# The modulation product of the second block: split float32r matmuls replaced by plain float32 matmuls on four 32-column strips

## The chip, the cores and the metric

The kernel runs on one core of a Trainium2 chip. The metric is the device time of one execution in microseconds (us); the time of a kernel is the median of its runs.

## What is computed

Two transformer-like blocks run one after the other on 256 tokens of width 1024, in float32. The second block has two layers, and each begins with a modulation: a vector `c` for the tokens and a vector `c_ctx` for the context are multiplied by a 1024 x 3072 matrix, and the result is cut into shift, scale and gate.

```python
for l in range(DEPTH):                                   # 2 layers
    mod_l = jax.nn.silu(c) @ w_ada[l] + b_ada[l]
    sh_l, sc_l, gt_l = jnp.split(mod_l[:, None, :], 3, axis=-1)
    mod_c = jax.nn.silu(c_ctx) @ w_ada[l] + b_ada[l]
    sh_c, sc_c, gt_c = jnp.split(mod_c, 3, axis=-1)
    h_l = _rmsnorm(x, g_pre[l]) * (1.0 + sc_l) + sh_l
    h_c = _rmsnorm(xc, g_pre[l]) * (1.0 + sc_c) + sh_c
    ...
    x = x + gt_l * _rmsnorm(out_l, g_post[l])
```

So the modulation is a product with two rows on the left and 24 MB of weights on the right (12 MB a layer). Nothing of the first block enters it, so it can be done at any time before the second block needs it.

## The kernel before

Matrix products run on TensorE with float32r operands. To keep precision, a weight tile of 1 MB (a unit: 128 partitions x 2048 floats) is loaded by one DMA into a buffer `raw` (three of these exist), ScalarE copies it as float32r (`hi`, L274) and VectorE subtracts that copy from the raw weights (`lo`, L275). Each half of a unit has its own `hi` and `lo` tile, of which four each exist. The activations are split in the same way, and `mm3` (L291 to L293) makes each product from three matmuls.

The modulation of one layer is the generator `ada` (L929). It works in 12 steps of 1 MB of weights, 24 for both layers: `product` (L937) takes 512 columns and 512 rows of `w_ada`, splits them as any other unit, and multiplies with `cvec`, four columns wide, namely hi and lo of the two vectors. These are eight matmuls, four with `lo` (L945) and four with `hi` (L946), each 512 columns wide with four stationary columns; the sum over the two halves of the rows and the bias are added by VectorE (L947). Eight steps make shift and scale; then small float32 matmuls with a selection matrix (L953) sum the rows and turn them into columns. Four steps make the gate, each second one followed by a float32 matmul with the selection matrix (L969), and the gate rows go to DRAM (L972).

What sets the order: these steps are pieces of filler. The first block (`block1`) yields a price of latency at each of its own steps, and the loop in `run` takes filler steps, each with a price in TensorE time, until the latency is paid. Eight modulation steps thus lie in the first 80 us among the first projections (reads of `in_e_w_in`), the other sixteen between 230 and 375 us, one after each unit of the first feed-forward (reads of `in_w_ff1` and `in_w_ff2`). A scheduler then fixes the order on each engine and the buffer that each tile gets; the order does not change during a run. All loads are issued by SyncE's queue (SP), in order: a load that waits for its buffer holds up the loads behind it.

Of the kernel before, what the change touches and what calls it, by code (L numbers as in the profile page):

```python
# [10 lines left out]
F32 = mybir.dt.float32  # L11
# [3 lines left out]
OP = mybir.AluOpType  # L15
# [12 lines left out]
# ---------------------------------------------------------------- constants that depend on shapes alone  # L28
# [26 lines left out]
# microseconds of other work that a step of the filler or of the background waits for, and its pace  # L55
# [26 lines left out]
def make_consts():  # L82
# [12 lines left out]
    # attention masks for [query, 256 keys] with queries 128..255  # L95
# [12 lines left out]
    # block 2 rope: [token, 128] in natural layout, halves of 32 inside each 64  # L108
# [10 lines left out]
    sel = np.zeros((100, 8), f)  # L119
    for q in range(4):  # L120
        for r in range(4):
            sel[32 * q + r, 2 * q + r % 2] = 1
# [4 lines left out]
# column-layout vectors (one value per partition), packed side by side  # L127
# [9 lines left out]
# row vectors that are spread over all partitions  # L137
# [10 lines left out]
def layout(inp):  # L148
    """Copies of the inputs in the layouts that the kernel loads; no arithmetic."""
# [22 lines left out]
    bada = np.zeros((2, 3, 4, 1024), np.float32)  # L172
    bada[:, :, 0] = a["b_ada_2"].reshape(2, 3, 1024)
    bada[:, :, 1] = a["b_ada_2"].reshape(2, 3, 1024)
    o["bada"] = bada
    for n in ("x", "e_w_in", "e_w_uq", "e_w_ukv", "e_w_out", "o_w_in", "o_w_out", "w_ff1", "w_ff2",
              "w_ple_gate", "w_ple_proj", "ctx_2", "w_ada_2", "w_in_2", "w_br_conv_2",
              "w_br_attn_2", "w_br_gla_2", "w_out_2", "g_post_2"):
# [8 lines left out]
class Pair:  # L187
    """x as hi + lo, both float32r, with the contraction index on partitions: [128, chunks, 256 tokens]."""
# [5 lines left out]
class Kern:  # L194
# [12 lines left out]
    # ------------------------------------------------------------ small helpers  # L207
# [24 lines left out]
    def load_consts(self):  # L232
# [7 lines left out]
        self.sel = g("sel", [100, 8])  # L240
# [39 lines left out]
    def tr_mm(self, ps, hi, lo, x, tick=False):  # L280
        """ps [128, 2, 256] = (columns of the unit) x (tokens)."""
# [38 lines left out]
    def gemm_tr(self, x, w, c0, cb, nk=8, width=256):  # L320
        """[256 columns of w as 2 x 128 partitions, 256 tokens]; cb(psum [128, 2, 256])."""
# [43 lines left out]
    def transposed(self, nat, nk, evac):  # L365
        """nat [128 tokens, 2, nk*128] -> evac(c0, n, psum [128, n, 256]) for runs of up to 2 chunks."""
# [9 lines left out]
    def square(self, h, ms, b, t, scr):  # L376
        """half b's part of the mean square of token tile t of h into ms[:, b, t]."""
# [10 lines left out]
    def raw_pair(self, h, gain):  # L388
        """h [128, 2, 1024] with a gain per column, transposed, as a pair: what follows scales by the rms norm's factor."""
# [1412 lines left out]
```

## Time and profile before

| | before |
|---|---|
| median of 3 runs | 2158.41 us (2156.14 to 2159.87) |
| profiled execution, span | 2158.8 us |
| TensorE (PE) busy | 2126.8 us, 99% |
| VectorE (DVE) busy | 1574.5 us, 73% |
| ScalarE (ACT) busy | 1167.1 us, 54% |
| splits of weights on DVE (L275), 620 | 748.3 us |
| splits of weights on ACT (L274), 620 | 641.5 us |
| matmuls of the modulation (L945, L946), 192 | 78.3 us of records, pipelined |

The profiled execution is as long as the median of the runs to within 0.4 us. How to read it: PE is the engine that is nearly always busy, but its records overlap: a matmul's record reaches to the end of its pipeline, so what one costs in a stream is the distance from its start to the next start, not the length of its record.

### The profile page before, as it was taken

To read this page: it belongs to the slowest core of one execution; us is meant where nothing else is said; L and a number is where in the kernel's file an instruction comes from. 1 tells how busy PE (TensorE), PEld (TensorE's weight loads), DVE (VectorE), ACT (ScalarE), POOL (GpSimd) and SP (SyncE) were. 2 spreads that over 40 slices of the span, in tenths; PEclk is the share of its full clock that TensorE was granted. 3 is DMA by queue.
4 is the path that set the end of the run, shared out by engine and by line. 5 is a ranking of instruction groups with operands and counts; after the bars stand their busy time and mean duration, and the time that the engine had idled before them with its cause. 6 is when DMAs were issued, how large, how long until landed. Compare 5 with 4: busy or idle time off the path is not lost.

```text
span 2158.8 us, 34589 instructions
## 1 busy us (share of the span) xinstructions
PE 2126.8 (99%) x13622; PEld 1881.5 (87%) x13622; DVE 1574.5 (73%) x2891; ACT 1167.1 (54%) x1838; POOL 9.2 (0%) x43
## 2 busy tenths in 40 slices
PE   7999999999999999999999999999999999999998
PEld 5788877888899988989998888889899988989997
DVE  7975787667766666898898577447878677667676
ACT  5754665455555445666565445434545445747553
POOL 0000000000000000000000000000000000000000
PEclk9999999999999999999999999999999999999999
DMA  8654687555435555754543343578876641425694
GB/s 262 221 167 150 220 276 261 186 177 191 149 106 174 195 189 182 248 185 134 187 132 117 112 136 121 166 241 277 282 237 193 206 139 58 141 84 164 204 314 175
DMA packets 290121, 397.06 MB, mean 184 GB/s; under 512 B 12658, under 2 KB 189138, under 8 KB 289574
## 3 DMA queue, kind: packets, MB, share of 16 engines
q1 hardware_dynamic: 289958, 394.85, 56.1%
q8 instruction: 107, 1.75, 0.3%
q14 instruction: 56, 0.46, 0.1%
HBM read 362.78 MB, written 32.03 MB: 183 GB/s over the span
## 4 chain that ended last, share of the span: by engine, by line
PE 90%; DVE 5%; ACT 3%; DMA 1%; issue 1%; SPq 0%; DVEq 0%; ACTq 0%
PE mm L292 25%; PE mm L293 25%; PE mm L291 25%; DVE wlo L275 2%; PE tp L1581 2%; PE at L1599 1%; PE at L1416 1%; PE at L1530 1%; PE mm L945 1%; PE mm L946 1%; PE at L576 1%; PE tp L1433 1%; ACT whi L274 1%; PE at L291 1%; PE tp L550 1%
## 5 line engine op out<-in xcount | busy, mean ns | idle before, releaser
L275 DVE TENSOR_TENSOR wlo<-raw,whi 128x1024 fp32r<-128x1024 f32 (+2 forms) x620 | 748.3, 1212 | 301.5 <-ACT whi L274 299.4
L274 ACT CAST whi<-raw 128x1024 fp32r<-128x1024 f32 (+2 forms) x620 | 641.5, 1041 | 472.9 <-PE mm L293 387.7
L291 PE MATMUL mm<-xh,wlo 128*128 128x256 f32 (+2 forms) x2048 | 621.1, 303 | 0.3 <-ACT xh L399 0.3
L292 PE MATMUL mm<-xl,whi 128*128 128x256 f32 (+2 forms) x2048 | 619.8, 303 | 0.9 <-DVE xl L400 0.9
L293 PE MATMUL mm<-xh,whi 128*128 128x256 f32 (+2 forms) x2048 | 618.3, 302 | 0.0
L291 PEld LDWEIGHTS mm<-xh,wlo 128*128 128x128 f32 (+1 forms) x2048 | 383.2, 187 | 16.1 <-ACT xh L399 0.5
L292 PEld LDWEIGHTS mm<-xl,whi 128*128 128x128 f32 (+1 forms) x2048 | 383.3, 187 | 15.5 <-DVE xl L400 1.1
L293 PEld LDWEIGHTS mm<-xh,whi 128*128 128x128 f32 (+1 forms) x2048 | 383.2, 187 | 14.2
L291 PE MATMUL mm<-whi,xl 128*128 128x512 f32 (+3 forms) x704 | 268.4, 383 | 3.1 <-ACT whi L274 2.9
L292 PE MATMUL mm<-wlo,xh 128*128 128x512 f32 (+3 forms) x704 | 269.4, 383 | 1.1 <-DVE wlo L275 1.1
L293 PE MATMUL mm<-whi,xh 128*128 128x512 f32 (+3 forms) x704 | 267.0, 380 | 0.0
L292 PE MATMUL mm<-pl,whi 128*128 128x256 f32 x576 | 160.9, 279 | 0.0
L293 PE MATMUL mm<-ph,whi 128*128 128x256 f32 x576 | 160.5, 279 | 0.0
L291 PE MATMUL mm<-ph,wlo 128*128 128x256 f32 x576 | 160.4, 279 | 0.0
L291 PEld LDWEIGHTS mm<-whi,xl 128*128 128x128 f32 x704 | 133.3, 190 | 29.6 <-ACT whi L274 4.3
L292 PEld LDWEIGHTS mm<-wlo,xh 128*128 128x128 f32 x704 | 133.7, 190 | 26.3 <-DVE wlo L275 2.4
L293 PEld LDWEIGHTS mm<-whi,xh 128*128 128x128 f32 x704 | 133.5, 190 | 24.8
L291 PE MATMUL mm<-whi,E 128*128 128x512 f32 (+1 forms) x292 | 115.3, 395 | 0.0
L293 PE MATMUL mm<-whi,E 128*128 128x512 f32 (+1 forms) x292 | 115.2, 395 | 0.0
L292 PE MATMUL mm<-wlo,E 128*128 128x512 f32 (+1 forms) x292 | 115.1, 394 | 0.0
L291 PEld LDWEIGHTS mm<-ph,wlo 128*128 128x128 f32 x576 | 108.4, 188 | 0.1
L292 PEld LDWEIGHTS mm<-pl,whi 128*128 128x128 f32 x576 | 108.2, 188 | 0.1
(454 smaller groups left out, 2902.6 us busy)
## 6 DMA issues: line engine op xcount, KB each, us to landing
raw<-in_w_in SPq DMA_DIRECT2D x130, 1024.0 KB
raw<-in_w_ff SPq DMA_DIRECT2D x64, 1024.0 KB
raw<-in_w_ada SPq DMA_DIRECT2D x24, 1024.0 KB
raw<-in_o_w_in SPq DMA_DIRECT2D x12, 1024.0 KB
raw<-in_w_br_conv SPq DMA_DIRECT2D x12, 1024.0 KB
raw<-in_w_br_attn SPq DMA_DIRECT2D x12, 1024.0 KB
raw<-in_w_br_gla SPq DMA_DIRECT2D x12, 1024.0 KB
raw<-in_w_out SPq DMA_DIRECT2D x12, 1024.0 KB
```

Of the source, the lines that this page charges most:

```text
L274: nc.scalar.copy(hi, src)
L275: nc.vector.tensor_sub(lo, src, hi.bitcast(F32))
L291: mm(ps, sl, mh, start=first, stop=False)
L292: mm(ps, sh, ml, start=False, stop=False)
L293: mm(ps, sh, mh, start=False, stop=last)
L550: nc.tensor.transpose(ps[:hd, j, t * P:(t + 1) * P], nat[:, t, h0 + j0 + j], self.ident)
L576: nc.tensor.matmul(bank[:, t * P:t * P + nk], qT[:, h, t * P:(t + 1) * P], kT[:, h, :nk], start=True, stop=True)
L945: nc.tensor.matmul(ps, a, lo[k], start=k == 0, stop=False)
L946: nc.tensor.matmul(ps, a, hi[k], start=False, stop=k == 3)
L1416: mm(ps[:, :nk], x[a], y[c], start=n == 0, stop=n == 2)
L1433: tr(tp[:, k * P:(k + 1) * P], e[:, t, k * P:(k + 1) * P], self.ident)
L1581: mm(ps[:, j], E[:, 0, j * P:(j + 1) * P], E[:, 1, j * P:(j + 1) * P], start=True, stop=True)
```

## The change

The weights of the modulation are no longer split. A step still loads 1 MB into `raw` (L945 of the changed file: 128 rows x 2048 columns for shift and scale, 256 rows x 1024 columns for the gate) and then issues four plain float32 matmuls (L949) that read `raw` itself, each with 512 columns moving and 32 stationary columns (`cpad`: two vectors and 30 columns of zeros). The four write to partitions 0, 32, 64 and 96 of one PSUM bank, so that each uses a 32-column strip of the array of its own. VectorE adds all 128 rows to a running sum in SBUF, once a step as before. The selection matrix is laid out for the new places; the gate of a layer has one product with it in place of two; bias and `g_post` come in as repeated rows. Filler prices and the number of steps are the same.

```diff
+        def quarters(k0, kc, c0, n, R, first):
+            raw = self.wp.tile([P, 2048], F32, name=f"raw{self.uid()}", tag="raw", bufs=3).rearrange("p (k n) -> p k n", k=kc)
+            nc.sync.dma_start(raw, w[k0 * P:(k0 + kc) * P, c0:c0 + n].rearrange("(k p) n -> p k n", p=P))
+            ps = self.mmbank()
+            for q in range(4):
+                k, b = divmod(q, n // 512)
+                mm(ps[32 * q:32 * q + 32], self.cpad[:, k0 + k], raw[:, k, b * 512:(b + 1) * 512], start=True, stop=True)
+            if first is None:
+                V.tensor_tensor(R, R, ps, op=OP.add)
+            else:
+                first(R, ps)
...
-        def product(part, half, rows):
-            c0 = half * 512
-            bias = ft("fb", [4, 512], 2)
-            nc.sync.dma_start(bias, i["bada"][l, part][:, c0:c0 + 512])
-            for k0 in (0, 4):
-                ps = self.mmbank()[:4]
-                hi, lo = self.unit(i["w_ada_2"][l], k0 * P, 4, part * D + c0, 512)
-                for k in range(4):
-                    a = self.cvec[:, k0 + k]
-                    nc.tensor.matmul(ps, a, lo[k], start=k == 0, stop=False)
-                    nc.tensor.matmul(ps, a, hi[k], start=False, stop=k == 3)
-                nc.vector.tensor_add(rows, ps, rows if k0 else bias)
-                yield 8 * MM512
-        for q in range(4):
-            yield from product(1 - q % 2, q // 2, R[32 * q:32 * q + 4])
+        for k in range(8):
+            quarters(k, 1, 0, 2048, R, None if k else lambda r, ps: V.tensor_tensor(r, ps, bias, op=OP.add))
+            yield 8 * MM512
...
-        for half in range(2):
-            c0 = half * 512
-            rows = ft("f2", [4, 512], 3)
-            yield from product(2, half, rows)
...
-            nc.tensor.matmul(ps[:2], self.sel[:4, :2], rows, start=True, stop=True)
...
+        for k in range(0, 8, 2):
+            quarters(k, 2, 2 * D, D, R, None if k else lambda r, ps: V.tensor_copy(r, ps))
+            yield 8 * MM512
+        bg, gp = (ft("f2", [4, 512], 3) for _ in range(2))
...
+        mm(ps, self.sel[:, 8:], R, start=True, stop=True)
```

On TensorE, between two units of the first feed-forward, there stood before (`mm` is a PSUM bank, `xh` and `xl` the split activations, `whi` and `wlo` the split weights):

```order
L293 MATMUL mm_2454<-xh,whi_0_128_2450 128x256
L945 MATMUL mm_2508<-wlo_0_0_2512,cvec 4x512
L946 MATMUL mm_2508<-whi_0_0_2511,cvec 4x512
L945 MATMUL mm_2508<-wlo_0_0_2512,cvec 4x512
L946 MATMUL mm_2508<-whi_0_0_2511,cvec 4x512
L945 MATMUL mm_2508<-wlo_2_0_2516,cvec 4x512
L946 MATMUL mm_2508<-whi_2_0_2515,cvec 4x512
L945 MATMUL mm_2508<-wlo_2_0_2516,cvec 4x512
L946 MATMUL mm_2508<-whi_2_0_2515,cvec 4x512
L291 MATMUL mm_2538<-xh,wlo_0_0_2531 128x256
```

At the same place there stands now (L297 to L299 are the three matmuls of `mm3` in the changed file):

```order
L298 MATMUL mm_2480<-xl,whi_0_128_2476 128x256
L299 MATMUL mm_2480<-xh,whi_0_128_2476 128x256
L949 MATMUL mm_2536<-raw_2534,cpad 32x512 x4
L297 MATMUL mm_2552<-xh,wlo_0_0_2545 128x256
L298 MATMUL mm_2552<-xl,whi_0_0_2544 128x256
```

Eight matmuls on split weights have become four that read the load's own buffer; the units of the first feed-forward stand around them as before.

On SP's queue in the same stretch the loads stood like this before, with what each waits for in brackets (`DVE` is VectorE's semaphore, `PE` TensorE's, `DMAHW` a transfer's):

```order
L264 DMA raw_2889<-in_w_ff 128x8x256 [waits DMAHW4_49,DVE_49]
L972 DMA gdram_135<-fb_325_2776 2x512 [waits DVE_49]
L939 DMA fb_327_2781<-in_bada 4x512 [waits DMAHW5_49]
L264 DMA raw_2956<-in_w_ada 128x4x512 [waits DMAHW6_49,DMAHW3_49,DVE_49]
L939 DMA fb_340_2953<-in_bada 4x512 [waits DMAHW1_49]
L264 DMA raw_2975<-in_w_ff 128x8x256 [waits DMAHW7_49,DVE_49]
L264 DMA raw_3040<-in_w_ada 128x4x512 [waits DMAHW0_49,DVE_49]
```

And now:

```order
L945 DMA raw_2765<-in_w_ada 128x2048 [waits DMAHW1_49,DVE_49,Activation_49]
L270 DMA raw_2773<-in_w_ff 128x8x256 [waits DMAHW2_49,PE_49]
L945 DMA raw_2837<-in_w_ada 128x2048 [waits DMAHW3_49,DVE_49,Activation_49]
L270 DMA raw_2845<-in_w_ff 128x8x256 [waits DMAHW6_49,PE_49]
L975 DMA f_384_3420<-in_bgate 4x512
L945 DMA raw_2909<-in_w_ada 128x2048 [waits DMAHW7_49,DVE_49]
L976 DMA f_385_3421<-in_gpost 4x512 [waits DMAHW4_49]
L270 DMA raw_2919<-in_w_ff 128x4x512 [waits DMAHW5_49,DMAHW0_49,PE_49]
```

The loads alternate as before, but a load that takes over the buffer of a modulation step now waits for TensorE, which reads that buffer, where it waited for VectorE's split. Eleven loads of first feed-forward weights wait for PE in the changed program, none before.

## Rows read from the trace of the kernel before

**Rows 1.** The page: span, TensorE's busy time, and the last-ended chain by engine

```profile
span 2158.8 us, 34589 instructions
PE 2126.8 (99%) x13622; PEld 1881.5 (87%) x13622; DVE 1574.5 (73%) x2891; ACT 1167.1 (54%) x1838; POOL 9.2 (0%) x43
...
PE 90%; DVE 5%; ACT 3%; DMA 1%; issue 1%; SPq 0%; DVEq 0%; ACTq 0%
```

**Rows 2.** Stretches: length, then busy time by engine, granted clock, DMA share, GB/s

```profile
22.00:80.00 58.00, 50.98 (x219) 32.73 (x219) 52.99 (x135) 39.04 (x59) 0.00 (x0) 0.91 0.75 247
24.00:32.00 8.00, 6.70 (x19) 2.45 (x20) 6.99 (x12) 6.39 (x10) 0.00 (x0) 0.62 0.55 168
40.00:46.00 6.00, 3.29 (x13) 0.97 (x12) 5.67 (x21) 4.99 (x15) 0.00 (x0) 1.00 0.99 335
46.00:54.00 8.00, 7.74 (x27) 5.69 (x28) 8.00 (x41) 3.80 (x4) 0.00 (x0) 0.79 0.85 278
230.00:375.00 145.00, 145.00 (x938) 116.07 (x937) 122.59 (x149) 88.25 (x108) 0.00 (x0) 1.00 0.79 258
```

**Rows 3.** The modulation's matmuls by line: count, ns min/median/max, first and last start

```profile
L945 PE MATMUL mm<-wlo,cvec x96: 387/396/629, 24.0 to 365.6; 128*4 128x512 f32 x96
...
L946 PE MATMUL mm<-whi,cvec x96: 387/397/629, 24.3 to 365.8; 128*4 128x512 f32 x96
```

**Rows 4.** TensorE in order of time, feed-forward and modulation: start, length, instruction

```profile
250.04 0.28 PE L293 MATMUL mm<-xh,whi 128*128 128x256 f32 x1
250.16 0.39 PE L945 MATMUL mm<-wlo,cvec 128*4 128x512 f32 x1
...
251.78 0.40 PE L946 MATMUL mm<-whi,cvec 128*4 128x512 f32 x1
252.01 0.28 PE L291 MATMUL mm<-xh,wlo 128*128 128x256 f32 x1
...
257.50 0.28 PE L293 MATMUL mm<-xh,whi 128*128 128x256 f32 x1
257.71 1.02 PE L969 MATMUL mm<-f,sel 4*2 4x512 f32 x2
258.66 0.40 PE L945 MATMUL mm<-wlo,cvec 128*4 128x512 f32 x1
```

**Rows 5.** The page's costliest groups: the splits, busy time and mean ns

```profile
L275 DVE TENSOR_TENSOR wlo<-raw,whi 128x1024 fp32r<-128x1024 f32 (+2 forms) x620 | 748.3, 1212 | 301.5 <-ACT whi L274 299.4
L274 ACT CAST whi<-raw 128x1024 fp32r<-128x1024 f32 (+2 forms) x620 | 641.5, 1041 | 472.9 <-PE mm L293 387.7
```

**Rows 6.** Plain float32 matmuls by line, columns as in rows 3

```profile
L969 PE MATMUL mm<-f,sel x8: 586/586/587, 257.7 to 372.2; 4*2 4x512 f32 x8
...
L1530 PE MATMUL at<-N,T x96: 377/380/484, 1002.8 to 1978.6; 128*128 128x256 f32 x96
```

**Rows 7.** TensorE in order of time, float32 (L1530) among float32r (L291 to L293)

```profile
1003.41 0.59 PE L1530 MATMUL at<-N,T 128*128 128x256 f32 x2
1003.65 0.47 PE L292 MATMUL mm<-xl,whi 128*128 128x256 f32 x1
1003.96 0.59 PE L1530 MATMUL at<-N,T 128*128 128x256 f32 x2
...
1005.06 0.28 PE L292 MATMUL mm<-xl,whi 128*128 128x256 f32 x1
1005.18 0.28 PE L293 MATMUL mm<-xh,whi 128*128 128x256 f32 x1
```

**Rows 8.** SP's queue in order of time: two loads of 1 MB

```profile
25.61 0.37 SPq L264 DMA_DIRECT2D raw<-in_w_ada  x1
...
247.80 0.37 SPq L264 DMA_DIRECT2D raw<-in_w_ff  x1
```

**Rows 9.** ScalarE in order of time: the casts that waited for those two loads

```profile
30.84 1.04 ACT L274 CAST whi<-raw 128x1024 fp32r<-128x1024 f32 x1 [1.47 <-DMA raw<-in_w_ada]
...
255.26 1.05 ACT L274 CAST whi<-raw 128x1024 fp32r<-128x1024 f32 x1 [0.96 <-DMA raw<-in_w_ff]
```

More of the change, by code (lines that the diff above doesn't have):

```diff
@@ L118, in make_consts @@
     c["c_invf"] = np.broadcast_to(inv, (P, 16)).copy()
-    sel = np.zeros((100, 8), f)
+    sel = np.zeros((P, 12), f)
     for q in range(4):
-        for r in range(4):
-            sel[32 * q + r, 2 * q + r % 2] = 1
+        for r in range(2):
+            sel[32 * q + r, 4 * (q % 2) + 2 * (1 - q // 2) + r] = 1
+            sel[32 * q + r, 8 + 2 * (q % 2) + r] = 1
     c["c_sel"] = sel
@@ L171, in layout @@
     o["dec"] = dec
-    bada = np.zeros((2, 3, 4, 1024), np.float32)
-    bada[:, :, 0] = a["b_ada_2"].reshape(2, 3, 1024)
-    bada[:, :, 1] = a["b_ada_2"].reshape(2, 3, 1024)
+    b6 = a["b_ada_2"].reshape(2, 6, 512)
+    bada = np.zeros((2, P, 512), np.float32)
+    for q in range(4):
+        for r in range(2):
+            bada[:, 32 * q + r] = b6[:, q]
     o["bada"] = bada
+    o["bgate"] = np.ascontiguousarray(np.repeat(b6[:, 4:], 2, axis=1))
+    o["gpost"] = np.ascontiguousarray(np.repeat(a["g_post_2"].reshape(2, 2, 512), 2, axis=1))
     for n in ("x", "e_w_in", "e_w_uq", "e_w_ukv", "e_w_out", "o_w_in", "o_w_out", "w_ff1", "w_ff2",
               "w_ple_gate", "w_ple_proj", "ctx_2", "w_ada_2", "w_in_2", "w_br_conv_2",
-              "w_br_attn_2", "w_br_gla_2", "w_out_2", "g_post_2"):
+              "w_br_attn_2", "w_br_gla_2", "w_out_2"):
         v = a[n]
@@ L239, in load_consts @@
         self.invf = g("invf", [P, 16])
[L240 removed]
+        self.sel = g("sel", [P, 12])
         self.rows = g("rows", [P, NROW])
@@ L931, in ada @@
         nc, i = self.nc, self.i
+        V, mm = nc.vector, nc.tensor.matmul
         ft = lambda tag, shape, bufs=1: self.fp.tile(shape, F32, name=f"{tag}{l}_{self.uid()}", tag=tag, bufs=bufs)
[L933 to L950 removed]
+        w = i["w_ada_2"][l]
+        def quarters(k0, kc, c0, n, R, first):
+            raw = self.wp.tile([P, 2048], F32, name=f"raw{self.uid()}", tag="raw", bufs=3).rearrange("p (k n) -> p k n", k=kc)
+            nc.sync.dma_start(raw, w[k0 * P:(k0 + kc) * P, c0:c0 + n].rearrange("(k p) n -> p k n", p=P))
+            ps = self.mmbank()
+            for q in range(4):
+                k, b = divmod(q, n // 512)
[4 more added lines that the diff above has]
+                first(R, ps)
+        R = ft("fr", [P, 512])
+        bias = ft("f2", [P, 512], 3)
+        nc.sync.dma_start(bias, i["bada"][l])
+        for k in range(8):
+            quarters(k, 1, 0, 2048, R, None if k else lambda r, ps: V.tensor_tensor(r, ps, bias, op=OP.add))
+            yield 8 * MM512
         ps = self.mmbank()[:, :32]
         for c in range(4):
[L953 removed]
+            mm(ps[:, 8 * c:8 * c + 8], R[:, c * P:(c + 1) * P], self.sel[:, :8], start=True, stop=True)
         p4 = ps.rearrange("p (c h a s) -> p a s h c", c=4, h=2, a=2)
@@ L957, in ada @@
         for s in range(2):
-            nc.vector.scalar_tensor_tensor(A[:, s], p4[:, 0, s], 1.0, g, op0=OP.add, op1=OP.mult)
-        nc.vector.tensor_copy(B, p4[:, 1])
+            V.scalar_tensor_tensor(A[:, s], p4[:, 0, s], 1.0, g, op0=OP.add, op1=OP.mult)
+        V.tensor_copy(B, p4[:, 1])
         yield 1
-        for half in range(2):
-            c0 = half * 512
-            rows = ft("f2", [4, 512], 3)
-            yield from product(2, half, rows)
-            gp = ft("fb", [4, 512], 2)
-            nc.sync.dma_start(gp, i["g_post_2"][l:l + 1, c0:c0 + 512].to_broadcast([4, 512]))
-            nc.vector.tensor_mul(rows, rows, gp)
-            ps = self.mmbank()
-            nc.tensor.matmul(ps[:2], self.sel[:4, :2], rows, start=True, stop=True)
-            g = ft("fb", [4, 512], 2)[:2]
-            nc.vector.tensor_copy(g, ps[:2])
-            nc.sync.dma_start(self.gdram[l][:, c0:c0 + 512], g)
+        R = ft("fr", [P, 512])
+        for k in range(0, 8, 2):
+            quarters(k, 2, 2 * D, D, R, None if k else lambda r, ps: V.tensor_copy(r, ps))
+            yield 8 * MM512
+        bg, gp = (ft("f2", [4, 512], 3) for _ in range(2))
+        nc.sync.dma_start(bg, i["bgate"][l])
+        nc.sync.dma_start(gp, i["gpost"][l])
+        ps = self.mmbank()[:4]
+        mm(ps, self.sel[:, 8:], R, start=True, stop=True)
+        V.tensor_tensor(bg, bg, ps, op=OP.add)
+        V.tensor_mul(bg, bg, gp)
+        for h in range(2):
+            nc.sync.dma_start(self.gdram[l][:, h * 512:(h + 1) * 512], bg[2 * h:2 * h + 2])
     def uid(self):
@@ L981, in ada_setup @@
         cv = self.cp.tile([P, 3, 8, 2], F32, name="cvf")
-        self.cvec = self.cp.tile([P, 8, 4], F32R, name="cvec")
+        self.cpad = self.cp.tile([P, 8, 32], F32, name="cpad")
+        nc.gpsimd.memset(self.cpad, 0.0)
         for s, n in enumerate(("c_2", "c_ctx_2")):
```

7 lines of the change are left out of this document (1 added, 6 removed).

## The prediction

> **What bounds the kernel now.** I read the page first: TensorE is busy 99% of the span, and the chain that ended last runs through it for 90% [rows 1]. So what counts is TensorE's time, piece by piece, and the few places where it waits. For these I read the table by stretches [rows 2]. From 230 to 375 us, where sixteen of the 24 modulation steps lie, TensorE is busy in all of the 145.00 us at full clock: a step there costs exactly its TensorE time, and what VectorE and ScalarE do beside it costs nothing. From 22 to 80 us, where the other eight lie, TensorE is busy 50.98 of 58.00 us. It stands for 7.0 us, and it runs slowly in two pieces: the granted clock averages 0.62 over 24 to 32 us and 0.79 over 46 to 54 us, that is part of each at 1.2 instead of 2.4 GHz, which loses 8 x 0.38 = 3.0 and 8 x 0.21 = 1.7 us. In that stretch VectorE is busy 52.99 of 58 us. So 11.7 us at most are to be had there by making data ready earlier.
>
> **What a step costs now.** The group by line gives 96 and 96 matmuls, eight for each of 24 steps [rows 3]. In order of time the first of a step starts at 250.16 us, 0.12 us after the feed-forward matmul before it, and the next unit starts at 252.01: 1.85 us a step [rows 4], 24 x 1.85 = 44.4 us. Going from whole-array matmuls to matmuls on the first strip and back costs nothing: 0.12 us is the usual step of a 256-column matmul, and 0.23 us (251.78 to 252.01) that of a 512-column one.
>
> **What a plain float32 matmul costs.** The program has four at L969, the trace eight records; 48 at L1530, and 96 records [rows 6]: each runs as two records, one after the other. In order of time a float32 matmul of 256 columns and one float32r matmul take 1003.96 - 1003.41 = 0.55 us, of which the float32r one takes 0.12 (1005.06 to 1005.18): 0.43 us for two records of 256 columns [rows 7]. A record of 512 columns thus takes 0.43 us. L969 agrees: two of them and their entry take 258.66 - 257.71 = 0.95 us [rows 4].
>
> A changed step has four such matmuls, eight records of 0.43 us, in the order first and second record of strip 0, first and second of strip 1, and so on. No row shows two strips at work at once, so I bound the step from both sides. **One after the other:** 8 x 0.43 = 3.44 us, 24 x 3.44 = 82.6, +38.2 us. **All four strips together:** only the two records of a strip follow each other, 0.86 us, 20.6 in all, -23.8 us. **Between:** strips work side by side, but records start in program order, and a strip holds one at a time. Then the second record of strip 0 waits for the first, and the first of strip 1, which could have begun, stands behind it. It starts together with that second record, and so on: five slots, 5 x 0.43 = 2.15 us, 51.6 in all, +7.2 us. I take the five slots, because in every row that I have TensorE starts its matmuls in the order of the program, and the order of the records is what the four strips have against them.
>
> The Trainium skill speaks on both halves of this. "TensorE: Matmul & The Clock Gate", Part 3 (packing small matmuls), says that matmuls on different column tiles overlap, and gives 2.38 times for three of them; the same section says that they start and end strictly in program order. No run here shows the first; by both together a step is the five slots above.
>
> **What else TensorE gains or loses.** The gate's products with the selection matrix go from four to two at 0.95 us [rows 4]: -1.9 us. The small product at L953 stays. The splits fall away: 48 on VectorE at 1.2 us and 48 on ScalarE at 1.0 us [rows 5], 58 and 50 us of engine time. For the sixteen steps in the full stretch this is worth nothing, since TensorE's own work covers it. In the first 80 us it helps: a step's matmuls wait for the load alone, and VectorE is free sooner for the projections' splits. I take -5 us of the 11.7. Not more, because the bytes to load stay the same and the DMA engines are already full in part of the stretch (share 0.99 from 40 to 46 us, 0.85 from 46 to 54) [rows 2]; the bounds are 0 and -11.7. VectorE's adds keep their number and their length of 512 columns.
>
> **A new wait.** A raw buffer used to come free when VectorE had split it, well ahead of TensorE. A modulation step's buffer now comes free when TensorE has used it. Eleven loads of feed-forward weights take over such a buffer, and for nine of them only one feed-forward unit and one step lie between that moment and their own first matmul: 5.6 us (48 matmuls from 252.01 to one step after 257.50 [rows 4]) plus 2.15 = 7.75 us. What must happen in that time: the load, then a cast of 1.05 and a subtraction of 1.2 us [rows 5, 9]. A load alone took from 25.61 to 30.84, 5.2 us; one that followed another took from 247.80 to 255.26, 7.5 us [rows 8, 9]. So the weights are ready after 7.5 to 9.7 us. At the middle, 8.6, TensorE waits 0.85 us, and only every second time: a wait also postpones the step behind it by no more than the next load needs, so the next unit finds its weights there. That is 9 x 0.42 = about +4 us, with bounds of 0 and +9. Queued behind each such load on SP is the next modulation step's load, which has a whole unit to spare.
>
> **The sum:** +7.2 - 1.9 - 5 + 4 = +4.3 us on the span of 2158.8: 2163.1. The median of the runs is 0.4 us below that span, so 2162.7, as **2163 us**. With the bounds of the last two terms this case reaches from 2152 (-6.4) to 2173 (+14.3).
>
> **Rivals.**
>
> *The strips do not overlap* (slower, decides if a record on another strip waits for the one before it). For it: no row shows an overlap, and all matmul records in the trace follow each other at the distance of their columns. Against it: nothing in the rows either, as all of the strip matmuls here use the same strip. +38.2 - 1.9 - 4 in the first 80 us, where part of the longer steps fills gaps; the new wait vanishes, since 5.6 + 3.44 = 9.0 us are enough for most loads. +32.3: 2191, from 2183 to 2198.
>
> *All four strips run together* (faster): a step of 0.86 us. That needs the second record of a strip to wait without holding up those behind it. -23.8 - 1.9 - 5, but then the time for a load shrinks to 5.6 + 0.86 = 6.5 us, so the wait is 2.1 us every second time, 9 x 1.07 = +9.6. -21.1: 2137, from 2125 to 2147. So even with perfect overlap about 40% of the saving in the steps would go into waits for weights. The Trainium skill's "TensorEngine Tiling (Array Packing)", Tiling Modes (key properties), has the rule that leads here: tiles are independent and can execute in parallel.
>
> *Five slots, and each change of strip mode empties the array.* The nearest row is L969, a product with another tile shape than its neighbours: about 0.09 us are lost before it (257.62, where the matmul before it ends its step, to 257.71) and as much behind it [rows 4]. Two such gaps in 24 steps are +4.3: 2167. Against it stands the step of today, which enters and leaves the first strip without a gap [rows 4]. The tiling page of the Trainium skill, in the same list, says that a change of mode drains the engine; this trace does not agree for the strip that is in use today.
>
> *The chances.* Five slots 0.45; no overlap 0.25; all together 0.22; five slots with gaps 0.08. A measurement of this kernel tells about 0.2%, 4.3 us, from no change, so same is 2154.1 to 2162.7. The five slots lie across that: 0.07 faster, 0.16 same, 0.22 slower. No overlap is slower, 0.25. All together is faster, 0.21, with 0.01 same. With gaps: 0.03 same, 0.05 slower. Sum: faster 0.28, same 0.20, slower 0.52. Cases of both signs hold most of the chance, so the range has to reach into both: 2138 to 2193 holds the five slots with and without gaps (0.53), about half of the fast case (0.11) and three quarters of the slow one (0.18). The likeliest case alone is 2152 to 2173.
>
> **What the profile after would show.** The distance from the first of a step's eight records to the next unit's first matmul, in the full stretch, decides between the cases: 2.15, 3.44 or 0.86 us; the starts of the second and third record tell whether strips run side by side. TensorE's idle time between 230 and 375 us, none today, shows the new wait, with feed-forward weights named as its cause, at nine units. TensorE's idle time and clock from 22 to 80 us show the gain at the start. The prediction is wrong if a step takes neither of these times, if the waits for weights exceed 9 us, or if the first stretch gains nothing or more than 11.7 us.

## The result and the profile after

The changed kernel takes 2133.97 us (median of 4 runs, 2131.45 to 2134.41) where the kernel before took 2159.14 us beside it (4 runs, 2156.14 to 2160.76): a ratio of 0.9883, 95% interval 0.9871 to 0.9895. It is faster by 1.2%; the forecast was 2163 us. The profiled execution has a span of 2132.1 us, 26.7 less than before [rows 1].

The page of the changed kernel: span, busy time, the chain that ended last by engine, and the two splits.

```profile
span 2132.1 us, 34406 instructions
...
PE 2092.7 (98%) x13618; PEld 1863.3 (87%) x13618; DVE 1516.2 (71%) x2837; ACT 1120.5 (53%) x1790; POOL 8.4 (0%) x42
...
PE 85%; DVE 6%; DMA 4%; ACT 4%; issue 1%; SPq 0%; DVEq 0%; ACTq 0%
...
L281 DVE TENSOR_TENSOR wlo<-raw,whi 128x1024 fp32r<-128x1024 f32 (+1 forms) x572 | 690.5, 1211 | 321.8 <-ACT whi L280 319.6
L280 ACT CAST whi<-raw 128x1024 fp32r<-128x1024 f32 (+1 forms) x572 | 592.0, 1041 | 487.1 <-PE mm L299 338.2
```

TensorE is busy 34.1 us less than in [rows 1], VectorE 58 and ScalarE 47 us less, the 48 splits each of [rows 5].

**A step.** TensorE in order of time in the first feed-forward of the changed kernel (start, length, instruction), the place that answers to [rows 4]:

```profile
243.08 0.28 PE L298 MATMUL mm<-xl,whi 128*128 128x256 f32 x1
243.19 0.28 PE L299 MATMUL mm<-xh,whi 128*128 128x256 f32 x1
243.40 1.06 PE L949 MATMUL mm<-raw,cpad 128*32 128x512 f32 x8
244.39 0.39 PE L297 MATMUL mm<-xh,wlo 128*128 128x256 f32 x1
244.61 0.28 PE L298 MATMUL mm<-xl,whi 128*128 128x256 f32 x1
```

From the last matmul ahead of a step to the next unit's first it was 252.01 - 250.04 = 1.97 us; it is 244.39 - 243.19 = 1.20 us. The matmul behind a step then takes 0.22 us to the next one instead of 0.12, and 0.09 of the 1.20 us pass ahead of the step (243.19 to 243.40 where 0.12 is usual). In all a step is 0.67 us shorter. From the first of the eight records to the next unit's first matmul it is 0.99 us: neither 2.15 nor 3.44 us. How many records stand open at once is told by a table of very short stretches, of this line's instructions alone (TensorE's busy time and count first):

```profile
243.39:243.42 0.03, 0.03 (x4) 0.03 (x4) 1.00 0.57 205
...
243.80:243.84 0.04, 0.04 (x4) 0.00 (x0) 1.00 0.81 256
```

Four records start within 30 ns, and the same four are still the only ones 0.4 us later; the other four follow them. These records don't name their strips; that all strips do their first record together and then all their second is read from what else the trace shows of the strips (in the part on why the prediction was wrong).

**The full stretch and the start.** The stretches that answer to [rows 2]:

```profile
22.00:80.00 58.00, 49.72 (x254) 35.21 (x253) 41.84 (x138) 27.42 (x50) 0.00 (x0) 0.91 0.76 266
...
230.00:375.00 145.00, 140.08 (x958) 111.99 (x957) 86.49 (x117) 58.84 (x76) 0.00 (x0) 1.00 0.77 267
```

VectorE and ScalarE have become free between 22 and 80 us (52.99 to 41.84 and 39.04 to 27.42 us), yet TensorE is still 8.3 of 58 us idle, at the same mean clock of 0.91. Between 230 and 375 us TensorE now stands idle for 4.9 us; before for none. One of these places, and the group of SP's waits for the first feed-forward (us, times, longest):

```profile
343.45 1.06 PE L949 MATMUL mm<-raw,cpad 128*32 128x512 f32 x8
345.75 0.38 PE L297 MATMUL mm<-xh,wlo 128*128 128x256 f32 x1 [1.24 <-DVE wlo L281]
```

```profile
SPq L270 <- PE mm L949: 52.6, 11, 6.5
```

Eleven feed-forward loads wait on SP until TensorE has read the modulation's buffer, and TensorE then waits for their split. That is the wait forecast. In the first feed-forward TensorE waits for splits of weights four times, 4.3 us in all.

**What does not fit.** Behind the first feed-forward there is no modulation step left, and still the remainder of the span is 11.5 us shorter (2158.8 - 457.0 against 2132.1 - 441.8). In the second feed-forward TensorE has the same 1169 records in both kernels:

```profile
659.80:842.80 183.00, 181.88 (x1169) 163.79 (x1168) 115.19 (x135) 89.31 (x113) 0.00 (x0) 1.00 0.56 184
```

```profile
643.00:822.10 179.10, 177.99 (x1169) 161.93 (x1168) 115.16 (x135) 89.35 (x113) 0.00 (x0) 1.00 0.57 188
```

The first row is of the kernel before, the second of the changed one. TensorE's busy time falls by 3.9 us with the same matmuls, at full clock, with VectorE and ScalarE as busy as before. The distance between the starts of two 256-column matmuls was 116.7 ns there (36 in a row took 4.20 us) and is 113.3 ns. Counted at one column per cycle of 2.4 GHz, 256 columns are 106.7 ns, so a matmul took 10.0 and now takes 6.7 ns beyond its columns; this surplus is called the pace below. So the product is not all that changed.

### The profile page after: what moved, and what is told of

The parts are those of the page before. It is cut to its first block, busy times and chain, and to the rows that moved or that the text cites. A ratio compares the mean times of both kernels' runs of the same rounds, so it can differ in the third digit from the quotient of the medians.

```text
span 2132.1 us, 34406 instructions
## 1 busy us (share of the span) xinstructions
PE 2092.7 (98%) x13618; PEld 1863.3 (87%) x13618; DVE 1516.2 (71%) x2837; ACT 1120.5 (53%) x1790; POOL 8.4 (0%) x42
## 4 chain that ended last, share of the span: by engine, by line
PE 85%; DVE 6%; DMA 4%; ACT 4%; issue 1%; SPq 0%; DVEq 0%; ACTq 0%
PE mm L298 24%; PE mm L299 24%; PE mm L297 24%; DVE wlo L281 2%; PE tp L1590 2%; DMA raw<-in_w_ff 1%; PE at L1608 1%; PE at L1425 1%; ACT whi L280 1%; PE at L1539 1%; PE at L582 1%; DMA lp<-scr01za 1%; PE tp L1442 1%; PE mm L949 1%; PE at L297 1%
## 5 line engine op out<-in xcount | busy, mean ns | idle before, releaser
L281 DVE TENSOR_TENSOR wlo<-raw,whi 128x1024 fp32r<-128x1024 f32 (+1 forms) x572 | 690.5, 1211 | 321.8 <-ACT whi L280 319.6
L280 ACT CAST whi<-raw 128x1024 fp32r<-128x1024 f32 (+1 forms) x572 | 592.0, 1041 | 487.1 <-PE mm L299 338.2
L297 PE MATMUL mm<-xh,wlo 128*128 128x256 f32 (+2 forms) x2048 | 619.0, 302 | 4.6 <-DVE wlo L281 4.3
L299 PE MATMUL mm<-xh,whi 128*128 128x256 f32 (+2 forms) x2048 | 614.7, 300 | 0.0
L297 PEld LDWEIGHTS mm<-xh,wlo 128*128 128x128 f32 (+1 forms) x2048 | 382.6, 187 | 29.1 <-DVE wlo L281 8.3
L299 PEld LDWEIGHTS mm<-xh,whi 128*128 128x128 f32 (+1 forms) x2048 | 383.6, 187 | 14.2
L297 PE MATMUL mm<-whi,xl 128*128 128x512 f32 (+3 forms) x704 | 267.1, 381 | 4.9 <-ACT whi L280 4.8
L299 PE MATMUL mm<-whi,xh 128*128 128x512 f32 (+3 forms) x704 | 265.9, 378 | 0.0
L297 PE MATMUL mm<-ph,wlo 128*128 128x256 f32 x576 | 162.7, 282 | 0.0
L299 PE MATMUL mm<-ph,whi 128*128 128x256 f32 x576 | 162.6, 282 | 0.0
L297 PEld LDWEIGHTS mm<-whi,xl 128*128 128x128 f32 x704 | 133.5, 190 | 31.8 <-ACT whi L280 8.0
L299 PEld LDWEIGHTS mm<-whi,xh 128*128 128x128 f32 x704 | 134.2, 191 | 23.1
L297 PE MATMUL mm<-whi,E 128*128 128x512 f32 (+1 forms) x292 | 113.5, 391 | 0.0
L299 PE MATMUL mm<-whi,E 128*128 128x512 f32 (+1 forms) x292 | 113.4, 388 | 0.0
L297 PEld LDWEIGHTS mm<-ph,wlo 128*128 128x128 f32 x576 | 109.2, 190 | 0.2 <-DVE wlo L281 0.2
```

The lines of the kernel that those rows point to most:

```text
L280: nc.scalar.copy(hi, src)
L281: nc.vector.tensor_sub(lo, src, hi.bitcast(F32))
L297: mm(ps, sl, mh, start=first, stop=False)
L299: mm(ps, sh, mh, start=False, stop=last)
```

## The experiments

The first idea was that two constants have grown (`cpad` by 896 bytes over the four-column tile it replaced, the selection matrix by 32), so that every tile behind them lies 928 bytes further on, and that TensorE reads faster from a multiple of 64 bytes.

**Tiles moved by 32 bytes, in both kernels; all tiles at multiples of 64 bytes.**

```diff
-        self.cpad = self.cp.tile([P, 8, 32], F32, name="cpad")
+        self.cpad = self.cp.tile([P, 264], F32, name="cpad")[:, :256].rearrange("p (k c) -> p k c", k=8)
```

> The changed kernel with one constant of the modulation given 32 bytes more than it uses, so that everything placed behind it, the split activations among it, lies 32 bytes further on; no instruction, wait or order differs. In the kernel before, the split activations begin 32 bytes past a multiple of 64, in the changed one at a multiple of 64, and here at 32 past again. Theory A (placement): of the 26.7 us gained, about 11 to 15 come from this alone; expected 2143 to 2149 us, and in the stretches of feed-forward and odd attention the step of a 512-column matmul goes from 223 to 229 ns back to 229 to 232, that of a 256-column one from 110 back to 114. Theory B (all of it comes from the product on four strips and from data made ready earlier): 2134 us, within 2.

```diff
-        cv = self.cp.tile([P, 3, 8, 2], F32, name="cvf")
+        cv = self.cp.tile([P, 56], F32, name="cvf")[:, :48].rearrange("p (a b c) -> p a b c", a=3, b=8)
```

> The kernel before with one constant given 32 bytes more than it uses, so that the split activations begin at a multiple of 64 bytes, as in the changed kernel; no instruction, wait or order differs. Theory A (placement): 2144 to 2148 us, a gain of 11 to 15 with no part of the change made. Theory B (the product on four strips is all): 2159 us, within 2.

The third kernel rounds the size of each tile up in the pools:

```diff
...
+        t = self.pool.tile([shape[0], -(-m // 16) * 16], dt, **k)[:, :m]
...
```

> The changed kernel with every tile's size rounded up to a multiple of 64 bytes, so that all tiles begin at one; nothing else differs. In the changed kernel the split activations of the first block begin at a multiple of 64, those of the branches of the second block and a part of its scratch 32 bytes past one, the other way round than in the kernel before; the stretch of the branches (1531.6 to 1627.5 us) is 1.6 us longer there than before. Theory A (placement): about 1.6 us back in each of three such stretches and some in the rest of the second block; expected 2120 to 2130 us. Theory B (placement does nothing): 2134 us, within 2.

Measured: the changed kernel moved by 32 bytes takes 2157.46 us (10 runs; ratio to the kernel before 0.9987, 0.9978 to 0.9996), 23.5 us more than unmoved. The kernel before, moved, takes 2162.24 us (10 runs; 1.0014, 1.0005 to 1.0024), and the kernel with all tiles aligned 2150.98 us (0.9954, 0.9938 to 0.9971). Placement matters more than expected, but the rule of 64 bytes fell: of the three kernels whose split activations begin at such a multiple, the changed one alone is fast. The same stretch as above, in the changed kernel moved by 32 bytes:

```profile
650.30:834.40 184.10, 182.99 (x1169) 164.81 (x1168) 115.19 (x135) 89.22 (x113) 0.00 (x0) 1.00 0.56 183
```

Five microseconds more than the 179.10 us of the same program. Two rows from its order in time, with 35 matmuls between them, and two from the unmoved kernel, with as many:

```profile
654.99 0.28 PE L299 MATMUL mm<-xh,whi 128*128 128x256 f32 x1
...
659.24 0.28 PE L297 MATMUL mm<-xh,wlo 128*128 128x256 f32 x1
```

```profile
647.70 0.28 PE L299 MATMUL mm<-xh,whi 128*128 128x256 f32 x1
...
651.78 0.28 PE L297 MATMUL mm<-xh,wlo 128*128 128x256 f32 x1
```

36 distances in 4.25 us (118.1 ns each) against 36 in 4.08 us (113.3). The second theory: what counts is how far the split activations lie from the split weights, since TensorE reads both.

**The split activations alone moved; everything moved.**

```diff
...
-        self.ones = cp.tile([98, 1], F32, name="ones")[96:98].to_broadcast([2, 256])
+        self.ones = self.op.tile([98, 1], F32, name="ones")[96:98].to_broadcast([2, 256])
...
```

For the first of the two kernels the pool of this tile of 32 bytes stands behind the split activations, for the second ahead of the weights, and the constant is enlarged as above.

> The changed kernel with one small constant placed behind the split activations instead of ahead of them: the split activations xh and xl (and three small constants) lie 32 bytes lower, the split weights and everything else stay where they are; no instruction, wait or order differs. After the run in which all behind the constants moved by 32 bytes (23.5 us slower than the changed kernel), three theories of the matmuls' pace. Theory C (it depends on the distance between the split weights and the split activations, which TensorE reads side by side): the pace changes wherever xh and xl are read, 16 to 20 ns beyond the columns' time in 512-column products and 10 to 12 in 256-column ones, and stays at 11.7 ns in the branches (1460 us on): 2142 to 2158 us. Theory D (it depends on where each lies by itself): the same. Theory E (a state that TensorE falls into and keeps): any pace, with changes in the branches too, where no address differs.

> The changed kernel with one small constant placed ahead of everything and another given 32 bytes more: every tile, split weights and split activations alike, lies 32 bytes further on, so that no distance between two of them differs from the changed kernel; no instruction, wait or order differs. Theory C (distance): the pace of the changed kernel in every stretch, 6.7 ns beyond the columns in the 256-column products of the second feed-forward; 2134 us, within 3. Theory D (place by itself): that of the run in which all behind the constants moved by 32 bytes, 11.7 ns there; 2150 to 2160 us. Theory E (state): neither has to hold.

Measured: 2154.3 us (6 runs; 0.9966, 0.9954 to 0.9979) with the activations alone moved, 2135.93 us (0.9883, 0.9863 to 0.9902) with everything moved, the changed kernel's ratio. The stretch, in this order:

```profile
649.30:831.10 181.80, 180.68 (x1170) 164.62 (x1169) 115.21 (x135) 89.24 (x113) 0.00 (x0) 1.00 0.56 185
```

```profile
648.50:827.60 179.10, 177.98 (x1170) 161.94 (x1168) 115.19 (x135) 89.28 (x113) 0.00 (x0) 1.00 0.58 188
```

In the branches, where no operand had moved against the weights, the kernel with the activations moved kept the changed kernel's pace (11.7 ns beyond the columns in both), as the theory of the distance demands.

**The kernel before, with the changed kernel's placement.** The same line of code as for the kernel before above, with `[P, 280]` for `[P, 56]`.

> The kernel before with one constant given 928 bytes more than it uses, so that the split activations and everything behind them lie exactly where they lie in the changed kernel, at the same distance from the split weights; no instruction, wait or order differs from the kernel before. Theory C (the matmuls' pace depends on the distance between the split weights and what they are multiplied with): the paces of the changed kernel, 6.7 instead of 10.0 ns beyond the columns in the 256-column products of the feed-forward, about 16 instead of 20 ns in the 512-column ones, 11.7 instead of 6.7 ns in the branches; in sum 16 to 19 us less: 2139 to 2144 us, without any part of the change made. The change itself is then worth what remains to the changed kernel's 2134 us, 6 to 10 us. If the pace comes from something else in the change: 2159 us, within 3.

Measured: 2146.03 us (4 runs; 0.9943, 0.9927 to 0.9958), span 2143.4 us, 2 us above the range expected. On the average of the program the paces are about those of the changed kernel (256-column products of block 1 8.4 ns beyond the columns against 8.0, branches 11.7 and 11.7, 512-column products 16.9 and 16.2). In the second feed-forward they are not, though this kernel's activations and weights lie where the changed kernel has them. The same stretch as above, and two of its matmuls with 35 between them:

```profile
652.80:834.30 181.50, 180.39 (x1169) 164.40 (x1168) 115.09 (x135) 89.24 (x113) 0.00 (x0) 1.00 0.56 185
```

```profile
657.55 0.28 PE L291 MATMUL mm<-xh,wlo 128*128 128x256 f32 x1
...
661.79 0.28 PE L292 MATMUL mm<-xl,whi 128*128 128x256 f32 x1
```

36 distances take 4.24 us (117.8 ns each, 11.1 beyond the columns), and TensorE's busy time is 2.4 us above the changed kernel's 177.99. So with the placement come 15.4 of the 26.7 us between the profiled executions, 13.1 of 25.2 us by the medians. What is left, **2143.4 - 2132.1 = 11.3 us of span** (12.1 us by the medians), bounds what the change itself is worth: 2.4 of it lie in this stretch, where the change has no part.

**All four matmuls on one strip.**

```diff
-                mm(ps[32 * q:32 * q + 32], self.cpad[:, k0 + k], raw[:, k, b * 512:(b + 1) * 512], start=True, stop=True)
+                mm(ps[:32], self.cpad[:, k0 + k], raw[:, k, b * 512:(b + 1) * 512], start=True, stop=True)
...
```

> The changed kernel with all four matmuls of a step on the first strip, each written over the one before it in the same 32 rows, and the sum taken over those 32 rows: three quarters of the product are lost, the matmuls, loads and waits stay in number and length. Theory A (the step of about 1.0 us comes from four strips that run at once): eight records one after the other, 3.44 us a step; 24 x 2.4 = 59 us more, less up to 5 us of waits for weights and up to 4 us of gaps at the start that the longer steps cover: 2183 to 2193 us. Theory B (a float32 matmul with 32 stationary columns is short by itself, strips or not): 2134 us, within 3.

Measured: 2173.04 us (4 runs; 1.0063, 1.0048 to 1.0078), 39 us more than the changed kernel and 10 less than the lower end expected. A step of it, in order of time, and how many records stand open in its first 0.3 us:

```profile
250.49 0.28 PE L299 MATMUL mm<-xh,whi 128*128 128x256 f32 x1
250.69 3.62 PE L949 MATMUL mm<-raw,cpad 128*32 128x512 f32 x8
254.25 0.39 PE L297 MATMUL mm<-xh,wlo 128*128 128x256 f32 x1
254.47 0.29 PE L298 MATMUL mm<-xl,whi 128*128 128x256 f32 x1
```

```profile
250.68:250.72 0.04, 0.03 (x1) 0.03 (x1) 1.00 1.22 384
250.72:251.00 0.28, 0.28 (x1) 0.11 (x2) 1.00 1.06 366
```

One record at a time, 0.43 us each, 3.56 us from the first to the next unit: the forecast's price of a record was right, and the strips are what makes eight of them take 0.99 us, 3.6 times less. From the matmul ahead of a step to the next unit it is 3.76 us against 1.20, so a step is 2.56 us longer. The time is below the expected one for two reasons. In the first feed-forward sixteen steps cost 41.0 us more, but the stretch is only 33.8 us longer (233.93 to 481.23 us against 228.35 to 441.85): the new wait, about 7 us, goes. At the start eight steps cost 20.5 us more, but the first feed-forward begins only 5.6 us later: most of their length falls into TensorE's waits.

**The new wait taken away.** For the sixteen steps inside the first feed-forward, the load is copied and TensorE reads the copies.

```diff
+            if self.ph == "ff0":
+                cs = [self.wp.tile([P, 1024], F32R, name=f"w{z}{self.uid()}", tag=f"w{z}", bufs=4).bitcast(F32) for z in ("hi", "lo")]
+                flat = raw.rearrange("p k n -> p (k n)")
+                nc.scalar.copy(cs[0], flat[:, :1024])
+                V.tensor_copy(cs[1], flat[:, 1024:])
...
```

> The changed kernel, in which ScalarE and VectorE, for the sixteen steps inside the first feed-forward, copy the load into the buffers of the split weights, and TensorE reads the copies: the load's buffer is free as soon as it is copied, as before the change. If the 4.9 us that TensorE stands idle between 228 and 442 us are the new wait (a feed-forward load that waits until TensorE has read the modulation's buffer), they fall below 1 us, and SP no longer waits there for TensorE; by itself 2129 to 2131 us. If they are something else (DMA too slow), they stay. The pace of the matmuls elsewhere may change as in the runs with moved tiles, by up to 20 us either way; so the verdict is read from the idle time in that stretch.

Measured: 2127.06 us (4 runs; 0.9843, 0.9827 to 0.9858), 7 us below the changed kernel, and every SP wait for TensorE's modulation matmuls in that stretch is gone. The first feed-forward from its first transposes to the next ones, in the kernel before with the changed kernel's placement, in the changed kernel, and with the copies (length, then busy time of TensorE, its weight loads, VectorE, ScalarE):

```profile
232.00:450.20 218.20, 218.20 (x1361) 180.60 (x1360) 167.85 (x196) 122.47 (x148) 0.00 (x0) 1.00 0.72 238
```

```profile
228.40:441.80 213.40, 208.48 (x1357) 172.30 (x1356) 128.26 (x159) 91.84 (x116) 0.00 (x0) 1.00 0.71 244
```

```profile
228.80:435.00 206.20, 206.20 (x1358) 171.93 (x1357) 140.75 (x176) 107.88 (x132) 0.00 (x0) 1.00 0.75 250
```

The wait costs 213.4 - 206.2 = 7.2 us, more than the 4.9 us that the page counts as idle. Without it the stretch is 12.0 us shorter than before at equal placement: 16 x 0.67 = 10.7 for the steps and 2.0 for the gate's products (below) make 12.7.

**The splits kept though nobody reads them.**

```diff
+            for k1 in range(2):
+                hi, lo = (self.wp.tile([P, 1024], F32R, name=f"w{z}{self.uid()}", tag=f"w{z}", bufs=4) for z in ("hi", "lo"))
+                src = raw.rearrange("p k n -> p (k n)")[:, k1 * 1024:(k1 + 1) * 1024]
+                nc.scalar.copy(hi, src)
+                V.tensor_sub(lo, src, hi.bitcast(F32))
```

> The changed kernel, in which the loads of the modulation are still split by ScalarE and VectorE as before the change, though nothing reads the halves. Theory A (the start gains because VectorE and ScalarE are free sooner, predicted at 5 us): the first feed-forward begins 3 to 6 us later than the 228.4 us of the changed kernel, and VectorE is busy some 53 us of 22 to 80 us again. Theory B (the start gains by the shorter steps alone, 8 x 0.7 = 5.3 us): it begins within 1.5 us of 228.4. The full stretch stays as it is in both, since VectorE has room there.

Measured: 2144.11 us (4 runs; 0.9919, 0.9904 to 0.9935), 10.1 us more than the changed kernel. All of it arises ahead of the first feed-forward, whose first transposes come at 239.01 instead of 228.35 us:

```profile
22.00:80.00 58.00, 44.37 (x214) 29.77 (x207) 50.15 (x134) 36.01 (x56) 0.00 (x0) 0.86 0.70 244
...
239.01 0.27 PE L402 MATMUL tp<-ident,h 128*128 128x128 f32 x1
```

```profile
228.35 0.38 PE L402 MATMUL tp<-ident,h 128*128 128x128 f32 x2
```

So it matters there that the splits are gone, by more than either theory said. This run does not tell apart the time of VectorE and ScalarE and the buffers of the split weights, which the unread halves take up too; the mean clock from 22 to 80 us is 0.86 here and 0.91 in the changed kernel.

**The distance used, and copies everywhere.** If the pattern repeats every 512 bytes, 480 bytes more ahead of the branches' operands give them the distance of the split activations.

```diff
-        S = T("S", [P, 8, 256])
+        S = T("S", [P, 2168])[:, :2048].rearrange("p (k n) -> p k n", k=8)
```

> The kernel with the copies (2127 us), in which one scratch tile of the second block's branches is given 480 bytes more, so that the branches' operands behind it lie 480 bytes further on, their distance from the split weights then being the same as that of the split activations of the first block when counted in 512 bytes; no instruction, wait or order differs. Theory C with a pattern that repeats every 512 bytes: 1700 matmuls of the branches at 6.7 to 8 instead of 11.6 ns beyond the columns, 6 to 8 us less: 2119 to 2122 us. If the pattern does not repeat so: 2127 us or up to 4 us more.

> The kernel with the copies and the 480 bytes once more, beside the one with copies everywhere. Theory A: 2124 us, within 2, and the paces of the branches at 6.7 ns as before. If the paces differ between executions of the same kernel, other values in this profile.

> The kernel with the copies and the 480 bytes, in which the eight steps ahead of the first feed-forward read copies too: there the load's buffer is then free when ScalarE and VectorE have copied it, at half the engine time of the old splits. In the changed kernel seven loads of that stretch wait for TensorE; here none. Theory A (the start gained little, 3.6 us at the same placement, because these new waits took back what the missing splits gave): the first feed-forward begins 2 to 5 us earlier than the 227.5 to 229 us of the kernels without. Theory B (VectorE and ScalarE are what the start waits for): it begins 2 to 6 us later, as the copies cost VectorE 8 and ScalarE 8 us there; in the run with full splits it began 10.6 us later. The rest stays: 2119 to 2130 us.

The third kernel differs from the first by one line, `if self.ph in ("even", "ff0"):`. Measured: 2124.2 us (4 runs; 0.9844, 0.9827 to 0.9862) and, once more, 2126.11 us (5 runs; 0.9846, 0.9832 to 0.9859); 2122.84 us (4 runs; 0.9836, 0.9821 to 0.985) with copies everywhere. The branches' pace came as forecast in the profile of the first: the same stretch of matmuls without the 480 bytes and with them:

```profile
1436.65:1454.39 17.74, 17.74 (x152) 17.74 (x151) 13.58 (x17) 8.95 (x11) 0.00 (x0) 1.00 0.77 250
```

```profile
1436.95:1453.95 17.00, 17.00 (x152) 17.00 (x151) 13.65 (x17) 9.00 (x11) 0.00 (x0) 1.00 0.85 270
```

The time gained by it, 1 to 3 us, is less than the 6 to 8 expected and within the intervals of the kernels with copies, which can't be told apart; all of them beat both kernels. In the profile of the second execution of the 480 bytes the branches went at 8.2 instead of 6.7 ns, and its span was 2127.5 instead of 2117.2 us: the same kernel does not always fall into the same pace. With copies everywhere the first transposes come at 224.55 us, 2.8 us ahead of the second execution's 227.34, though VectorE has 7.6 us more to do between 22 and 80 us:

```profile
22.00:80.00 58.00, 49.77 (x263) 35.15 (x264) 49.65 (x150) 37.05 (x62) 0.00 (x0) 0.97 0.74 264
...
224.55 0.38 PE L402 MATMUL tp<-ident,h 128*128 128x128 f32 x2
```

```profile
22.00:80.00 58.00, 49.81 (x254) 35.53 (x247) 42.09 (x137) 27.74 (x51) 0.00 (x0) 0.91 0.75 264
...
227.34 0.27 PE L402 MATMUL tp<-ident,h 128*128 128x128 f32 x1
```

So loads that waited for TensorE had cost the start about that much or more. The mean clock is 0.97 here and 0.91 there; how much of the 2.8 us came by way of the clock was not tried.

## Why the prediction was wrong, step by step

**The step of 2.15 us failed, and with it the term of +7.2.** It measured 0.99 us. The forecast let the first record of strip 1 stand behind the second record of strip 0, which waits for its strip. In the trace a matmul that waits for its strip does not hold up those behind it on other strips. This is seen where the gate's product with the selection matrix, on strip 0, runs directly into a step, in the run with copies (L985 is that product; strips 0 and 1 of the step read `whi`, strips 2 and 3 `wlo`):

```profile
263.82 0.59 PE L985 MATMUL mm<-fr,sel 128*4 128x512 f32 x1
263.84 0.62 PE L956 MATMUL mm<-whi,cpad 128*32 128x512 f32 x1
263.84 0.62 PE L956 MATMUL mm<-wlo,cpad 128*32 128x512 f32 x2
264.25 0.59 PE L985 MATMUL mm<-fr,sel 128*4 128x512 f32 x1
264.29 0.59 PE L956 MATMUL mm<-whi,cpad 128*32 128x512 f32 x1
264.30 0.60 PE L956 MATMUL mm<-wlo,cpad 128*32 128x512 f32 x2
264.68 1.02 PE L956 MATMUL mm<-whi,cpad 128*32 128x512 f32 x2
```

Three of the step's matmuls start at 263.84 us, beside the product on strip 0. The fourth, on strip 0 and in the program ahead of those three, does both its records from 264.68 us on, 0.43 us after that product's second record began. So here each strip goes on by itself, and neither records nor matmuls on different strips wait for each other's turn. The Trainium skill's "TensorE: Matmul & The Clock Gate", Part 3 (packing small matmuls), has the span of matmuls on different tiles as the duration of one plus some 4 ns for each further tile; the trace agrees in that the four of a step start within 30 ns. The same part's sentence on strict order, which the forecast used against the overlap, does not hold here: the strip 0 matmul starts 0.84 us after three that stand behind it.

The rival "all four strips together" had the mechanism, with 0.86 us. What it lacked is entry and exit: 0.09 us ahead of the step, 0.99 - 0.86 = 0.13 us more until the next unit starts, and 0.10 us behind that unit's first matmul. With these 0.32 us a step is 0.67 us shorter, not 0.99. So for 24 steps 24 x 0.67 = 16.1 us fewer of TensorE's time stand where the forecast had 7.2 us more. The last rival had taken 0.18 us for a change of strip mode from [rows 4]. On one strip the three are the same (0.08, 0.12 and 0.10 us), so they don't come from the number of strips. The Trainium skill's "TensorEngine Tiling (Array Packing)", Tiling Modes (key properties), says that such a change drains the engine; the gap ahead of the step agrees, but the float32r step before the change was on a strip too and showed none.

**The gate's products, -1.9 us, were right.** Four took 0.95 us each [rows 4]; of the two that remain one takes 0.82 us (with copies, ten records from 263.82 us on in 1.81 instead of a step's 0.99) and one 0.95: -2.0 us.

**The new wait was right in kind and place.** It was put at +4 us beside a step of 2.15 us and at +9.6 beside one of 0.86; it took 7.2 us beside 1.20, and on one strip about 7 us went with it.

**The start was counted twice.** The forecast added 5 us for earlier data to the savings of the eight steps there, 8 x 0.99 in the rival. At equal placement the first feed-forward begins 232.04 - 228.35 = 3.7 us earlier, everything included; the row of the kernel before with the changed kernel's placement:

```profile
232.04 0.27 PE L396 MATMUL tp<-ident,h 128*128 128x128 f32 x1
```

That the splits are gone is worth about 10 us in the changed kernel (splits kept), but the loads' wait for TensorE, which the forecast looked for in the first feed-forward alone, costs here too: about 2.8 us or more (copies everywhere). Of the steps' own 8 x 0.67 = 5.3 us most seems lost in TensorE's other waits: on one strip 20.5 us of longer steps put the first feed-forward off by 5.6 us, and by that share 5.3 us would be worth 1.4, an estimate.

**What no step of the forecast had:** the grown constants move every tile behind them, and the matmuls' pace with it, in the whole program. That is 15.4 of the 26.7 us. The remaining 11.3 us are 3.7 at the start, 4.7 in the first feed-forward (-10.7 for the steps, -2.0 for the gate, +7.2 for the wait come to -5.5), and 2.9 behind it, where executions of one kernel differ as much. So 8.4 us can be put down to the change; the 2.9, of which 2.4 lie in the second feed-forward, can't. The measured time lies in the range of the rival "all together", 2125 to 2147, for which the prediction shows no working, by luck: its sum was -21.1 us, the same causes gave at most -11.3, and placement, which it did not have, gave -15.4.

## What to carry to other kernels

Small products in plain float32 on four column strips run at once here, whatever their order in the program, but a step pays for entering and leaving them, and a buffer that TensorE reads straight from the load is held until TensorE gets there: copy it if the next load is due. Before a change of about 1% is put down to its mechanism, run the kernel before with the new placement of the tiles (some bytes more in one constant); here that alone was about half of the gain. Compare more than one stretch and execution, since the pace of the same matmuls on the same tiles can differ. Where all matmuls of a long program read two families of tiles, their distance is worth a sweep.

## What was not expected of the hardware

The time from one matmul's start to the next, less its columns at 2.4 GHz, averaged over all pairs of like matmuls with less than 40 ns of it, goes with the distance of the activations from the split weights, counted in 512 bytes, in 14 profiles of 13 kernels and whatever the tile. Each entry is the range over profiles of such averages:

| bytes (mod 512) | 256 columns, weights stationary | 512 columns, weights moving |
|---|---|---|
| 32, 64 | - | 20.0 ns |
| 128 | 12.1 ns | 19.2 |
| 160 | 11.3 | 20.0 |
| 192 | 7.7 to 8.8 | 15.9 to 17.4 |
| 224 | 11.6 to 11.7 | 19.9 to 20.0 |
| 256 | 13.3 | 13.5 to 13.9 |
| 288 | 10.2 | 19.8 to 20.0 |
| 320 | 9.6 to 10.8 | 20.0 |
| 352, 384 | 13.3 (352) | 20.9, 19.3 |
| 448 | - | 15.7 to 16.8 |
| 480 | - | 20.0 |

The kernel before had 288 for block 1 and 320 for the branches, the changed one 192 and 224. That the distance counts, and not the place of either tile, is shown by the runs that moved one family or both; that it repeats after 512 bytes rests on the 480 bytes and on the table; why it counts is open. It is not all: an average can hide two paces at one distance. The changed kernel, which did 36 products in 4.08 us at the beginning of its second feed-forward, takes 4.24 us for 36 near its end, on the same tiles:

```profile
764.92 0.28 PE L297 MATMUL mm<-xh,wlo 128*128 128x256 f32 x1
...
769.16 0.28 PE L297 MATMUL mm<-xh,wlo 128*128 128x256 f32 x1
```

That is 6.7 and 11.1 ns beyond the columns, and the entry of 192 bytes is mostly a mixture of these two; so is the lower one at 320, of the kernel before, whose branches went at 6.7 ns from 1450 to 1515 us and at 11.1 ns in their two later stretches. With 512 columns, in the second mixing part of block 1, again at 192, the changed kernel went at 15.6 ns and the kernel with one strip at 20.0, each for 60 us without a break. What sets such a state, and why one kernel's executions can differ in it, was not tried. The Trainium skill's "SBUF — State Buffer", section "SBUF: two separate sides", says that TensorE's port never waits on anyone. That is said of contention between engines, which no run here tests, and not of the two operands of one matmul. The runs that move tiles differ by up to 23.5 us, and none of them shows where inside TensorE or the memory the time goes.
